# x's transposes for the second FFN in float32r, from copies of x, among its plain tiles

## The chip, the cores and the metric

One core of one Trainium2 chip runs the kernel in one launch. The metric is the device time of the launch in microseconds. The time before is the median of three runs. Four engines compute side by side, each with an instruction stream of its own in fixed order: PE multiplies, DVE and ACT work on elements, POOL issues DMAs with accumulation here; SP issues DMAs only.

## The reference

A residual layer on 512 tokens of 1024 channels, in float32:

```python
for l in range(DEPTH):
    x = x + 0.5 * swiglu_ffn(rmsnorm(x, ffn1_norm[l]), ffn1_w_gate[l], ffn1_w_up[l], ffn1_w_down[l])
    x = x + hybrid_mixer(rmsnorm(x, mix_norm[l]), w_in[l], q_norm[l], k_norm[l], rel_bias[l],
                         pool_w[l], pool_scale[l], w_out[l])
    x = x + 0.5 * swiglu_ffn(rmsnorm(x, ffn2_norm[l]), ffn2_w_gate[l], ffn2_w_up[l], ffn2_w_down[l])
    x = rmsnorm(x, final_norm[l])
return x
```

`swiglu_ffn` is `(silu(h @ w_gate) * (h @ w_up)) @ w_down` with 2816 hidden channels; `rmsnorm` divides each token by the root of its mean square and multiplies by a gain.

## The kernel before

Channels lie on the 128 partitions and tokens along the row, so x is eight tiles of 128 channels by 512 tokens, kept in SBUF. Float32 operands are split into two float32r parts, `hi` (rounded) and `lo` (the rest): `split` (lines 146 to 155) makes `hi` on ACT (line 148) and `lo` on DVE (line 149). `mm3` (lines 189 to 194) then issues three products, hi·hi at line 192, lo·hi at 193 and hi·lo at 194. The weight loads of `weights` (line 185) go out on SP, which waits at its front when a target buffer is not free.

The three parts FFN1, mixer and FFN2 follow one another. An FFN's first half is `ffn_up`. Its hidden channels are 22 tiles of 128; the first five in the order are plain, the later ones go through a Strassen scheme. The first two plain tiles are done together, gate and up of both in four PSUM banks, in four steps over the input channels called kp0 to kp3: each loads one weight tile (128 x 1024), splits it and issues 2 x 4 x 3 = 24 products. Plain tiles three and four follow one at a time, each as a gate (j = 0) and an up half (j = 1) of 24 products; these halves are called f2j0, f2j1, f3j0 and f3j1 below.

The FFN's rmsnorm is not applied to x ahead of the products. The products use x times its gain; the factor per token, `rb`, is multiplied in when the banks are emptied. It comes from `acc`, the sum of squares over tiles, which is complete when the last x tile has got the mixer's output (adds at line 1455, squares at line 304, sums at line 305). `Norm.finish` splits `acc` (lines 148 and 149), sums it over the partitions with two products against ones on PE (line 336), and goes on: square root on ACT (line 356), load of the table for silu (line 223), then on DVE `v` (line 358), reciprocal (line 359), and a Newton step (lines 360, 361, 363) that ends in `rb`. It is called within `tc.high_priority()` at the last of the kp steps; outside the manual schedules a scheduler puts each engine's stream in order when the program is built, and this priority moves its instructions forward.

FFN2's second half makes its output with tokens on the partitions, so it needs x by token, too. For that, x is transposed at the start of FFN2 (lines 1506 to 1515): eight times, four 128x128 transposes on PE from x's float32 tiles into a PSUM bank (line 1510), a copy to SBUF on ACT (line 1514), a store to the scratch `x_d` in DRAM on SP (line 1515). The second half reads it back from there much later.

`down.begin` opens the SBUF tiles for the hidden values (`acts`, one per group of hidden tiles); `open(range(G - 3))` opens all but the last three groups at once. `todo` and `piece` spread a list of small DVE and ACT tasks for the Strassen blocks among the plain tiles.

Of the kernel before, what the change touches and what calls it, by code (L numbers as in the profile page):

```python
# [1 line left out]

# [6 lines left out]
F32 = mybir.dt.float32  # L9
F32R = mybir.dt.float32r  # L10
I32 = mybir.dt.int32
AF = mybir.ActivationFunctionType
ALU = mybir.AluOpType
# [3 lines left out]
P = 128  # L17
D = 1024
S = 512
KD = D // P  # L20
NT = S // P
# [48 lines left out]
def layer(  # L70
# [31 lines left out]
    nc = tc.nc  # L102

    const = ctx.enter_context(tc.tile_pool(name="const", bufs=1))
# [13 lines left out]
    def name(what):  # L118
        n_tiles[0] += 1
        return f"{what}_{n_tiles[0]}"  # L120

    def temp(dtype=F32):
        return tpool.tile([P, S], dtype, tag="t", name=name("t"))

    def bank(tag="mm", bufs=4):
        return ps.tile([P, S], F32, tag=tag, name=name(tag), bufs=bufs)

    def abank():
        return bank("a", 4)
# [9 lines left out]
    def piece(n=1):  # L139
        for _ in range(min(n, len(todo))):  # L140
            what, *args = todo.pop(0)
            what(*args)
# [36 lines left out]
    def weights(src, parts=1):  # L179
        n = src.shape[-1]  # L180
        raw = raw_tile()
        hi, lo = part_tiles()
        for i in range(parts):
            part = slice(i * n // parts, (i + 1) * n // parts)
            nc.sync.dma_start(raw[:, part], src[:, part])  # L185
            split(raw[:, part], hi[:, part], lo[:, part])
        return hi, lo

    def mm3(acc, a, b, start, stop, further=False):

        more = dict(skip_group_check=True) if further else {}
        nc.tensor.matmul(acc, a[0], b[0], start=start, stop=False, **more)  # L192
        nc.tensor.matmul(acc, a[0], b[1], start=False, stop=False, **more)  # L193
        nc.tensor.matmul(acc, a[1], b[0], start=False, stop=stop, **more)  # L194

    def cut(pair, lo, n):
        if isinstance(pair[0], list):
            pair, lo = [z[lo // S] for z in pair], lo % S
        return pair[0][:, lo : lo + n], pair[1][:, lo : lo + n]


    def residual_tiles():
        pairs = [xpool.tile([P, 2 * S], F32, tag=f"x{k}", name=name("x")) for k in range(KD // 2)]
        return [pairs[k // 2][:, k % 2 * S : (k % 2 + 1) * S] for k in range(KD)]

    x = residual_tiles()
    x_d = dram.tile([2 * NT, P, S], F32, name="x_d")
# [3 lines left out]
    ident = const.tile([P, P], F32, name="ident")  # L211
# [3 lines left out]
    table = const.tile([P, 2], F32, name="table")  # L215
    nc.vector.memset(ones, 1.0)
    nc.vector.tensor_copy(ones_r, ones)
    eps = table[:, 1:2]
    nc.vector.memset(eps, EPS)

# [204 lines left out]
            ]  # L425


    def ffn_up(norm, wA, down, loaded):

# [6 lines left out]
        def evacuate(f, gate, up):  # L438
            g = temp()
            nc.vector.tensor_tensor(g, gate, norm.rb, op=ALU.mult)  # L440
            sg = temp()
            nc.scalar.activation(sg, g, AF.Silu)

            nc.vector.tensor_tensor(sg, sg, norm.rb, op=ALU.mult)
            down.place(f, up, sg)
            down.sums(f)
            return sg
# [3 lines left out]
        for kp in range(KD // 2):  # L451
# [10 lines left out]
            for kk in range(2):  # L462
                k = 2 * kp + kk
# [76 lines left out]
        for n, f in enumerate(down.order[2 : PLAIN - 1], 2):  # L540
            banks = []
            for j in range(2):
                wj = weights(wA[2 * f + j])
                acc = bank()
                for k in range(KD):
                    mm3(acc, cut(wj, k * P, P), norm.h[k], k == 0, k == KD - 1)
                banks.append(acc)
                piece(4)
            down.make_sums(evacuate(f, *banks), 2)
            if not loaded:  # L550
                next(consts)
        piece(len(todo) - 4)

        n, f = PLAIN - 1, down.order[PLAIN - 1]
        wj = [weights(wA[2 * f + j]) for j in range(2)]
# [43 lines left out]
        with tc.manual_schedule(engines={E.PE, E.DVE, E.Activation, E.SP}):  # L599
            last_silu = last_place = last_sums = nothing  # L600
            for n in range(PLAIN, KF):
                f = down.order[n]
                acc, up_lo, up_hi = bank()[:, :HT], bank()[:, :HT], abank()[:, :HT]
                u, z, sg = temp(), temp(), temp()
# [67 lines left out]
    groups = [(k, min(2, KH - k)) for k in range(0, KH, 2)]  # L672
    G = len(groups)

    class Down:
# [37 lines left out]
        def begin(self, pool):  # L713
            self.pool, self.acts = pool, []
            self.raws, self.parts, self.pairs = {}, {}, {}
            self.n_products, self.loads, self.loads_from = 0, [], 4
            self.open(range(G - 3))
            rooms[:] = [
                z for tag in ("ra", "rb") for z in ((wpool, "raw", RAW, 1024), (pool, tag, RAW, 2 * S))
            ]  # L720
            part_rooms[:] = [(wpool, HILO)] * HILO + [(pool, 1)]
# [116 lines left out]
    n1, n2, n3 = Norm(0), Norm(1), Norm(2)  # L838
# [11 lines left out]
    def block2(i, g):  # L850
# [6 lines left out]
    down1 = Down(  # L857
        order1, lambda f: (f % KH, f // KH), block1, RATES
    )
    down2 = Down(list(range(KF)), lambda f: (f // 2, f % 2), block2, RATES)  # L860

    with tc.tile_pool(name="act1", bufs=1, reuse_waits="tile") as apool:
        down1.begin(apool)
        ffn_up(n1, wA1, down1, loaded=False)
        p1, p5, p6 = whole(bank), whole(bank), whole(abank)

        with tc.manual_schedule(engines={mybir.EngineType.SP}):
            for g in range(G):
                down1.product(p6, g, S2, T2)
                down1.product(p1, g, A11, B11)  # L870
                down1.product(p5, g, S1, T1)
                if g == 0:

                    x[:] = residual_tiles()
                    down1.loads, down1.loads_from = [(x[k], xT[k]) for k in range(KD)], 19
        with tc.manual_schedule(engines={mybir.EngineType.SP}):
            p7 = whole(abank)
            u2 = halved(p6)

            y = [down1.acts[i // 2][:, i % 2].rearrange("p k c -> p (k c)") for i in range(2 * NT)]  # L880
            down1.product(p7, 0, S3, T3)
            for tt in range(2):
                scaled(u2[tt], p1[tt][0][0], 0.5, u2[tt], ALU.subtract)
                scaled(y[NT + 2 + tt], p5[tt][0][0], 0.5, u2[tt])
            for g in range(G):
                if g + 1 < G:
                    down1.product(p7, g + 1, S3, T3)
                down1.product(p5, g, S4, B22, further=True)

            def add(d):  # L890

                tp = bank() if d >= KD // 2 else abank()
                for t in range(NT):
                    nc.tensor.transpose(  # L894
                        tp[:, t * P : (t + 1) * P],
                        y[d // 4 * NT + t][:, d % 4 * P : (d % 4 + 1) * P], ident,
                    )
                nc.vector.tensor_tensor(x[d], x[d], tp, op=ALU.add)
                n2.add(d)

            for tt in range(2):
                todo.append((scaled, y[NT + tt], p5[tt][0][0], -0.5, u2[tt], ALU.subtract))
                todo.append((scaled, y[NT + 2 + tt], p7[tt][0][0], 0.5, y[NT + 2 + tt]))
            for g in range(G):
                down1.product(p1, g, A12, B21, further=True)
                piece()
            todo.extend((add, d) for d in range(KD // 2, KD))
            for tt in range(2):
                nc.scalar.activation(y[tt], p1[tt][0][0], AF.Copy, scale=0.5)
            ahead = down1.operands(0, A22, T4, -1.0)  # L910
            for g in range(G):
                a, w = ahead
                if g + 1 < G:
                    ahead = down1.operands(g + 1, A22, T4, -1.0)
                down1.mms(p7, g, a, w, further=True)
                piece()
            for tt in range(2):
                scaled(y[2 + tt], p7[tt][0][0], -0.5, u2[tt], ALU.subtract)
            for d in range(KD // 2):
                add(d)  # L920
        rooms[:] = [(wpool, "raw", RAW, 1024)]
# [581 lines left out]
    with tc.tile_pool(name="act2", bufs=1, reuse_waits="tile") as apool:  # L1503
        down2.begin(apool)

        for half in range(2):
            for t in range(NT):
                tp = abank()
                for j in range(4):
                    nc.tensor.transpose(  # L1510
                        tp[:, j * P : (j + 1) * P], x[4 * half + j][:, t * P : (t + 1) * P], ident
                    )
                z = temp()
                nc.scalar.copy(z, tp)
                nc.sync.dma_start(x_d[half * NT + t], z)
        ffn_up(n3, wA2, down2, loaded=True)
        xt = [hpool.tile([P, S], F32, tag="h", name=name("xt")) for _ in range(2 * NT)]
        rooms.extend((xpool, f"x{i}", 1, 2 * S) for i in range(KD // 2))
        gb = [temp(), temp()]
# [90 lines left out]
        for tt in range(2):  # L1610
            scaled(u2[tt], p1[tt][0][0], 0.5, u2[tt], ALU.subtract)
            residual(1, 2 + tt, p5[tt][0][0])
            for i in (2 + tt, NT + tt, NT + 2 + tt):
                op = ALU.subtract if i < NT + 2 else ALU.add
# [128 lines left out]
```

## Time and profile before

| what | value |
|---|---|
| median of 3 runs | 838.43 us (838.31 to 838.51) |
| the profiled execution | 838.57 us |
| its span, first to last instruction | 836.7 us |
| busy: PE, DVE, ACT, POOL | 99%, 85%, 60%, 18% |
| granted PE clock, mean | 0.997 |
| DMA, mean | 189 GB/s |

The profile is of one execution; its times in us start at the span's beginning. `a<-ident,x` reads "tile a, made from ident and x". "[0.51 <-ACT t L1514]" behind a row means that the engine stood idle for 0.51 us ahead of it, until ACT's work on t at line 1514. A row with x16 joins 16 neighbours of one line. PEld is the loading of PE's weights, which runs beside its products; SPq is SP issuing.

### The profile page before, as it was taken

The page shows a single profiled execution, that of the slowest core. Times are in us where ns is not written, and L with a number is a line of the kernel's source. Part 1 is how long each engine was busy: PE and PEld are TensorE (multiplying, and loading weights), DVE is VectorE, ACT ScalarE, POOL GpSimd, SP SyncE. Part 2 cuts the span into 40 slices and gives each one's busy share as a digit, 9 for nine tenths or more (in the row PEclk, how much of TensorE's full clock was granted, in tenths as well). Part 3 has the DMA queues.
Part 4 walks back from the last instruction along what each step waited for, and adds up shares of the span by engine and source line. Part 5 has one row for each costly group of instructions (what it writes and reads, how often), then busy time and mean ns, then how long its engine had stood idle before and what let it go on. Part 6 is the DMA issues. An engine that isn't in the chain of part 4 may idle for free.

```text
span 836.7 us, 14334 instructions
## 1 busy us (share of the span) xinstructions
PE 827.8 (99%) x5288; PEld 742.3 (89%) x5288; DVE 711.1 (85%) x1156; ACT 501.7 (60%) x859; POOL 153.1 (18%) x212
## 2 busy tenths in 40 slices
PE   9999999999999999999999999999999999999996
PEld 7889999999988888887888888889999999988885
DVE  7999999899897678767879668989889999887896
ACT  8446555665675656558747746455566555756573
POOL 0312211222073000102011000311121121132600
PEclk9999999999999999999999999999999999999998
DMA  8667788888679963332222119547877888689922
GB/s 301 194 186 200 175 211 252 191 208 205 198 239 276 336 219 111 108 110 89 75 70 64 66 55 304 173 126 215 211 214 216 217 203 209 231 268 340 325 87 101
DMA packets 77686, 158.52 MB, mean 189 GB/s; under 512 B 7200, under 2 KB 30256, under 8 KB 77232
## 3 DMA queue, kind: packets, MB, share of 16 engines
q1 hardware_dynamic: 54528, 110.93, 39.4%
q0 software_dynamic: 22656, 46.14, 26.3%
q8 instruction: 41, 0.67, 0.3%
q10 hardware_dynamic: 432, 0.54, 0.2%
q14 instruction: 29, 0.24, 0.1%
HBM read 153.38 MB, written 50.34 MB: 243 GB/s over the span
## 4 chain that ended last, share of the span: by engine, by line
PE 97%; DMA 1%; DVE 1%; SPq 0%; ACT 0%; issue 0%; DVEq 0%; ACTq 0%
PE mm L192 23%; PE mm L193 23%; PE mm L194 23%; PE a L193 8%; PE a L192 8%; PE a L194 8%; PE a L1303 1%; PE a L1239 1%; PE a L1291 1%; DMA raw<-in_wA_dram 1%; PE a L1510 0%; PE a L1161 0%; PE a L309 0%; PE a L894 0%; PE mm L894 0%; SPq L185 0%
## 5 line engine op out<-in xcount | busy, mean ns | idle before, releaser
L149 DVE TENSOR_TENSOR wlo<-raw,whi 128x1024 fp32r<-128x1024 f32 (+2 forms) x115 | 124.4, 1089 | 26.0 <-ACT whi L148 25.5
L148 ACT CAST whi<-raw 128x1024 fp32r<-128x1024 f32 (+2 forms) x115 | 107.5, 945 | 62.4 <-PE mm L193 16.9
L193 PE MATMUL mm<-ha,whi 128*128 128x256 f32 x408 | 112.9, 277 | 0.0
L192 PE MATMUL mm<-ha,whi 128*128 128x256 f32 x408 | 112.9, 277 | 0.0
L194 PE MATMUL mm<-ha,wlo 128*128 128x256 f32 x408 | 112.9, 277 | 0.0
L591 ACT ACTIVATE t<-mm 128x256 f32<-128x256 f32 x102 | 39.1, 384 | 115.2 <-PE mm L194 112.5
L495 DVE TENSOR_TENSOR wlo<-wsum,whi 128x1024 fp32r<-128x1024 f32 x68 | 83.0, 1221 | 11.2 <-PE mm L194 7.9
L732 POOL COPY mark<-t 128x1 f32<-128x1 f32 x44 | 17.5, 398 | 392.8 <-DVE t L640 242.5
L193 PEld LDWEIGHTS mm<-ha,whi 128*128 128x128 f32 x408 | 76.6, 188 | 0.1
L192 PEld LDWEIGHTS mm<-ha,whi 128*128 128x128 f32 x408 | 76.6, 188 | 0.1
L194 PEld LDWEIGHTS mm<-ha,wlo 128*128 128x128 f32 x408 | 76.6, 188 | 0.0
L192 PE MATMUL mm<-hhi,whi 128*128 128x512 f32 x192 | 75.7, 397 | 0.1
L194 PE MATMUL mm<-hhi,wlo 128*128 128x512 f32 x192 | 74.9, 392 | 0.0
L193 PE MATMUL mm<-hlo,whi 128*128 128x512 f32 x192 | 74.7, 390 | 0.0
L734 POOL DMA_DIRECT2D wsum<-in_wB_dram x72 | 71.1, 1101 | 10.4 <-issue 7.1
L490 ACT CAST whi<-wsum 128x1024 fp32r<-128x1024 f32 x68 | 67.9, 1047 | 3.3 <-DVE wsum L521 3.1
L193 PE MATMUL mm<-wlo,ah 128*128 128x512 f32 x176 | 68.7, 390 | 0.0
L194 PE MATMUL mm<-whi,ah 128*128 128x512 f32 x176 | 68.6, 390 | 0.0
L192 PE MATMUL mm<-whi,ah 128*128 128x512 f32 x176 | 68.5, 390 | 0.0
L495 DVE TENSOR_TENSOR wlo<-raw,whi 128x512 fp32r<-128x512 f32 x68 | 62.2, 951 | 0.0
L490 ACT CAST whi<-raw 128x512 fp32r<-128x512 f32 x68 | 56.3, 827 | 3.7 <-issue 2.5
L192 PE MATMUL a<-whi,ah 128*128 128x512 f32 (+1 forms) x154 | 55.8, 362 | 0.0
(229 smaller groups left out, 2399.0 us busy)
## 6 DMA issues: line engine op xcount, KB each, us to landing
raw<-in_wA_dram SPq DMA_DIRECT2D x136, 256.0 KB, 4.0
wsum<-in_wB_dram POOLq DMA_DIRECT2D x60, 512.0 KB, 7.2
raw<-wsum SPq DMA_DIRECT2D x40, 512.0 KB, 4.8
raw<-in_wB_dram SPq DMA_DIRECT2D x30, 512.0 KB, 7.2
wsum<-wsum POOLq DMA_DIRECT2D x20, 512.0 KB, 5.6
raw<-in_wA_dram SPq DMA_DIRECT2D x19, 512.0 KB, 4.8
x<-in_xT_dram SPq DMA_DIRECT2D x16, 256.0 KB, 9.0
raw<-in_wQK_dram SPq DMA_DIRECT2D x8, 512.0 KB, 3.5
```

What stands on the lines that cost most here:

```text
L148: nc.scalar.copy(hi, src)
L149: nc.vector.tensor_tensor(lo, src, hi.bitcast(F32), op=ALU.subtract)
L192: nc.tensor.matmul(acc, a[0], b[0], start=start, stop=False, **more)
L193: nc.tensor.matmul(acc, a[0], b[1], start=False, stop=False, **more)
L194: nc.tensor.matmul(acc, a[1], b[0], start=False, stop=stop, **more)
L490: nc.scalar.copy(hi, src)
L495: nc.vector.tensor_tensor(lo, src, hi.bitcast(F32), op=ALU.subtract)
L591: nc.scalar.activation(dst, src, AF.Copy, scale=scale)
L732: nc.gpsimd.tensor_copy(mark, after[:, 0:1])
L734: nc.gpsimd.dma_start(self.rows(i, g), self.rows(self.terms[i][at], g), **(dict(accum_op=ALU.add) if at else {}),)
L1239: nc.tensor.matmul(banks[i][:, at : at + n], qT[pair][0][a][rows, t * P : (t + 1) * P], kT[pair][0][b][rows, :n], start=a + b == 0, stop=a ...
L1291: nc.tensor.transpose(tp[:, n : n + P], prob[h, t][:, j * P : (j + 1) * P], ident)
```

## The change

The transposes read float32r copies of x instead of x itself. Eight DMAs on SP copy x within SBUF, bits unchanged, into two tiles `xr`, which lie in the room of the hidden values' groups 1 and 2; those groups are opened only after the plain tiles (`open(range(1))` at the start, `open(range(1, G - 3))` behind the loop), in FFN1 as well. The transposes are no longer issued at the start of FFN2 but two groups at a time at the end of each half of plain tiles three and four, through the list `further` of `ffn_up`. Each group is four float32r transposes against a float32r identity, then the copy on ACT and the store on SP. For the first group four more transposes run in float32 from the same copy; the difference of the two results times 1e9 is added to the first, on DVE.

```diff
--- before.py
+++ after.py
@@ -1,4 +1,5 @@
 from contextlib import ExitStack, nullcontext
+from functools import partial
 
 import concourse.bass as bass
 import concourse.tile as tile
@@ -215,6 +216,8 @@
     table = const.tile([P, 2], F32, name="table")
     nc.vector.memset(ones, 1.0)
     nc.vector.tensor_copy(ones_r, ones)
+    ident_r = const.tile([P, P], F32R, name="ident_r")
+    nc.vector.tensor_copy(ident_r, ident)
     eps = table[:, 1:2]
     nc.vector.memset(eps, EPS)
 
@@ -425,7 +428,7 @@
             ]
 
 
-    def ffn_up(norm, wA, down, loaded):
+    def ffn_up(norm, wA, down, loaded, further=()):
 
 
 
@@ -546,10 +549,14 @@
                     mm3(acc, cut(wj, k * P, P), norm.h[k], k == 0, k == KD - 1)
                 banks.append(acc)
                 piece(4)
+                for _ in range(2):
+                    if further:
+                        further.pop(0)()
             down.make_sums(evacuate(f, *banks), 2)
             if not loaded:
                 next(consts)
         piece(len(todo) - 4)
+        down.open(range(1, G - 3))
 
         n, f = PLAIN - 1, down.order[PLAIN - 1]
         wj = [weights(wA[2 * f + j]) for j in range(2)]
@@ -714,7 +721,7 @@
             self.pool, self.acts = pool, []
             self.raws, self.parts, self.pairs = {}, {}, {}
             self.n_products, self.loads, self.loads_from = 0, [], 4
-            self.open(range(G - 3))
+            self.open(range(1))
             rooms[:] = [
                 z for tag in ("ra", "rb") for z in ((wpool, "raw", RAW, 1024), (pool, tag, RAW, 2 * S))
             ]
@@ -861,7 +868,7 @@
 
     with tc.tile_pool(name="act1", bufs=1, reuse_waits="tile") as apool:
         down1.begin(apool)
-        ffn_up(n1, wA1, down1, loaded=False)
+        ffn_up(n1, wA1, down1, False)
         p1, p5, p6 = whole(bank), whole(bank), whole(abank)
 
         with tc.manual_schedule(engines={mybir.EngineType.SP}):
@@ -1503,17 +1510,37 @@
     with tc.tile_pool(name="act2", bufs=1, reuse_waits="tile") as apool:
         down2.begin(apool)
 
-        for half in range(2):
-            for t in range(NT):
-                tp = abank()
+        xr = [
+            apool.tile([P, 4, S], F32R, tag=f"acts{groups[g][0]}", name=name("xr")) for g in (1, 2)
+        ]
+        for k in range(KD):
+            nc.sync.dma_start(xr[k // 4][:, k % 4].bitcast(F32), x[k])
+
+        def by_token(half, t):
+
+            tp = abank()
+            for j in range(4):
+                nc.tensor.transpose(
+                    tp[:, j * P : (j + 1) * P].bitcast(F32R), xr[half][:, j, t * P : (t + 1) * P],
+                    ident_r,
+                )
+            z = temp()
+            if (half, t) == (0, 0):
+                whole_passes = abank()
                 for j in range(4):
                     nc.tensor.transpose(
-                        tp[:, j * P : (j + 1) * P], x[4 * half + j][:, t * P : (t + 1) * P], ident
+                        whole_passes[:, j * P : (j + 1) * P],
+                        xr[half][:, j, t * P : (t + 1) * P].bitcast(F32), ident,
                     )
-                z = temp()
+                differ = temp()
+                nc.scalar.copy(differ, whole_passes)
+                nc.vector.tensor_tensor(differ, tp, differ, op=ALU.subtract)
+                nc.vector.scalar_tensor_tensor(z, differ, 1e9, tp, op0=ALU.mult, op1=ALU.add)
+            else:
                 nc.scalar.copy(z, tp)
-                nc.sync.dma_start(x_d[half * NT + t], z)
-        ffn_up(n3, wA2, down2, loaded=True)
+            nc.sync.dma_start(x_d[half * NT + t], z)
+
+        ffn_up(n3, wA2, down2, True, [partial(by_token, i // NT, i % NT) for i in range(2 * NT)])
         xt = [hpool.tile([P, S], F32, tag="h", name=name("xt")) for _ in range(2 * NT)]
         rooms.extend((xpool, f"x{i}", 1, 2 * S) for i in range(KD // 2))
         gb = [temp(), temp()]
```

Line numbers of the changed kernel are higher by 1 to 7: 148 becomes 149, 336 becomes 339, 358 to 363 become 361 to 366, 1455 becomes 1462. What the scheduler makes of it stands in the engines' streams.

**PE, from the last products of the mixer** (`mm<-m`) into FFN2 (`mm<-hhi`), before:

```order
L192 MATMUL mm_5941<-m_5806,whi_5902 128x512
L193 MATMUL mm_5941<-m_5807,whi_5902 128x512
L194 MATMUL mm_5941<-m_5806,wlo_5903 128x512
L1510 MATMUL a_6043<-ident,x_3123 128x128 x2
L1510 MATMUL a_6043<-ident,x_3124 128x128 x2
L1510 MATMUL a_6051<-ident,x_3123 128x128 x2
L1510 MATMUL a_6051<-ident,x_3124 128x128 x2
L1510 MATMUL a_6059<-ident,x_3123 128x128 x2
L1510 MATMUL a_6059<-ident,x_3124 128x128 x2
L1510 MATMUL a_6067<-ident,x_3123 128x128 x2
L1510 MATMUL a_6067<-ident,x_3124 128x128 x2
L192 MATMUL mm_6107<-hhi_5896,whi_6112 128x512
```

and after the change, from the last three products of kp0 (`whi_6058`) into kp1 (`whi_6088`):

```order
L193 MATMUL mm_6056<-hhi_5917,whi_6058 128x512
L194 MATMUL mm_6056<-hlo_5918,whi_6058 128x512
L195 MATMUL mm_6056<-hhi_5917,wlo_6059 128x512
L1523 MATMUL a_6261<-ident_r,xr_6043 128x128 x4
L1531 MATMUL a_6267<-ident,xr_6043 128x128 x4
L1523 MATMUL a_6277<-ident_r,xr_6043 128x128 x4
L1523 MATMUL a_6320<-ident_r,xr_6043 128x128 x4
L193 MATMUL mm_6053<-hhi_5947,whi_6088 128x512
L194 MATMUL mm_6053<-hlo_5948,whi_6088 128x512
L193 MATMUL mm_6054<-hhi_5947,whi_6088 128x512
L194 MATMUL mm_6054<-hlo_5948,whi_6088 128x512
```

The transposes have left the front; the first 16 (12 in float32r, four in float32) stand between kp0 and kp1, and kp1 starts with eight products that need only `whi_6088`, four with `wlo_6089` behind. The other 20 stand in groups of four at the ends of f2j1 (one), f3j0 (two) and f3j1 (two).

**DVE and ACT around the norm of FFN2.** DVE before; `acc_5900` is the sum of squares, `wlo_6143` belongs to kp1 and `wlo_6173` to kp2:

```order
L149 TENSOR_TENSOR t_6208<-acc_5900,t_6207 128x512
L149 TENSOR_TENSOR wlo_6143<-raw_6141,whi_6142 128x1024
L149 TENSOR_TENSOR wlo_6173<-raw_6171,whi_6172 128x1024
L358 TENSOR_SCALAR t_6215<-a_6209 128x512
L359 RECIPROCAL t_6216<-t_6214 128x512
L149 TENSOR_TENSOR wlo_6203<-raw_6201,whi_6202 128x1024
L360 TENSOR_TENSOR t_6214<-t_6216 128x512
L149 TENSOR_TENSOR wlo_6282<-raw_6280,whi_6281 128x1024
```

DVE after the change; `t_6154` is the low part of the sum of squares, `wlo_6089` belongs to kp1:

```order
L150 TENSOR_TENSOR t_6154<-acc_5902,t_6153 128x512
L361 TENSOR_SCALAR t_6161<-a_6155 128x512
L362 RECIPROCAL t_6162<-t_6160 128x512
L363 TENSOR_TENSOR t_6160<-t_6162 128x512
L364 SCALAR_TENSOR_TENSOR t_6161<-t_6160,t_6161 128x512
L150 TENSOR_TENSOR wlo_6089<-raw_6087,whi_6088 128x1024
L366 SCALAR_TENSOR_TENSOR rb_6169<-t_6161,t_6162 128x512
L150 TENSOR_TENSOR wlo_6119<-raw_6117,whi_6118 128x1024
```

Two `wlo` stood between the norm's split and its first step; now four steps of the norm stand ahead of kp1's `wlo`. ACT before (the copy is the last of eight; `whi_6142` is kp1's):

```order
L1514 COPY t_6104<-a_6099 128x512
L148 CAST t_6207<-acc_5900 128x512
L148 CAST whi_6142<-raw_6141 128x1024
L148 CAST whi_6172<-raw_6171 128x1024
L356 ACTIVATE t_6214<-a_6209,table 128x512
L148 CAST whi_6202<-raw_6201 128x1024
L223 ACT_TABLE_LOAD
L223 ACTIVATE table<-t_6214 128x1
L148 CAST whi_6281<-raw_6280 128x1024
```

and after:

```order
L307 ACTIVATE t_6034<-x_3128 128x512
L149 CAST t_6153<-acc_5902 128x512
L359 ACTIVATE t_6160<-a_6155,table 128x512
L226 ACT_TABLE_LOAD
L226 ACTIVATE table<-t_6160 128x1
L149 CAST whi_6088<-raw_6087 128x1024
L149 CAST whi_6118<-raw_6117 128x1024
```

The copies are gone from here, and the square root and the table load now stand ahead of kp1's `whi_6088`.

**SP, from the first weights of FFN2** (`raw_6111` is kp0's, `raw_6141` kp1's, `raw_6201` kp3's), before:

```order
L185 DMA raw_6111<-in_wA_dram 128x1024
L185 DMA raw_6171<-in_wA_dram 128x1024
L185 DMA raw_6280<-in_wA_dram 128x1024
L185 DMA raw_6141<-in_wA_dram 128x1024
L185 DMA raw_6201<-in_wA_dram 128x1024
L1515 DMA x_d<-t_6048 128x512
L1515 DMA x_d<-t_6056 128x512
L1515 DMA x_d<-t_6064 128x512
```

and after (`raw_6087` is kp1's):

```order
L186 DMA raw_6057<-in_wA_dram 128x1024
L186 DMA raw_6117<-in_wA_dram 128x1024
L186 DMA raw_6226<-in_wA_dram 128x1024
L1517 DMA xr_6043<-x_3125 128x512 x2
L1517 DMA xr_6043<-x_3126 128x512 x2
L1517 DMA xr_6044<-x_3127 128x512 x2
L1517 DMA xr_6044<-x_3128 128x512 x2
L186 DMA raw_6087<-in_wA_dram 128x1024
L186 DMA raw_6147<-in_wA_dram 128x1024
```

The eight copies of x stand ahead of kp1's and kp3's weights, where the stores of x by token stood behind them; the stores now stand among the later weights.

## The prediction

> **What bounds the kernel now.** I read the page's busy table first, then the shares of the chain that ended last, and then a table by stretches of time.
>
> ```profile
> PE 827.8 (99%) x5288; PEld 742.3 (89%) x5288; DVE 711.1 (85%) x1156; ACT 501.7 (60%) x859; POOL 153.1 (18%) x212
> PE 97%; DMA 1%; DVE 1%; SPq 0%; ACT 0%; issue 0%; DVEq 0%; ACTq 0%
> ```
>
> TensorE (PE) is busy for 99% of the span and is 97% of the chain. So what counts is PE's own work and any wait put in front of it. The stretches around the start of the second FFN, and a sum over everything behind it, with the columns length, PE, PEld, DVE, ACT, POOL busy, granted clock, DMA share, GB/s:
>
> ```profile
> 502.00:510.00 8.00, 7.92 (x51) 6.50 (x50) 4.22 (x8) 7.84 (x15) 0.00 (x0) 1.00 0.86 314
> 510.00:520.00 10.00, 10.00 (x45) 8.26 (x44) 10.00 (x9) 5.83 (x7) 0.00 (x0) 1.00 0.96 320
> ```
>
> ```profile
> sum 313.00, PE 313.00 PEld 289.44 DVE 278.92 ACT 178.97 POOL 66.15; mean PE 62.60 PEld 57.89 DVE 55.78 ACT 35.79 POOL 13.23
> ```
>
> The last line sums five stretches from 515 to 828: PE is busy for all 313.00 us. Nothing there can absorb a delay: what PE loses near 510 arrives at the end in full. DVE is 10.00 of 10 busy from 510 to 520, so an instruction put ahead of another on DVE there delays the second by its whole length.
>
> **PE in the stretch that changes.** PE's timeline (start, length, what):
>
> ```profile
> 501.69 0.39 PE L194 MATMUL mm<-m,wlo 128*128 128x512 f32 x1
> 501.92 1.91 PE L1510 MATMUL a<-ident,x 128*128 128x128 f32 x16
> 503.58 0.48 PE L192 MATMUL mm<-hhi,whi 128*128 128x512 f32 x1
> 503.90 0.40 PE L193 MATMUL mm<-hlo,whi 128*128 128x512 f32 x1
> ...
> 505.06 0.66 PE L1510 MATMUL a<-ident,x 128*128 128x128 f32 x4
> 505.47 0.48 PE L194 MATMUL mm<-hhi,wlo 128*128 128x512 f32 x1
> 505.79 1.47 PE L1510 MATMUL a<-ident,x 128*128 128x128 f32 x12
> ...
> 509.76 0.44 PE L336 MATMUL a<-t,ones_r 128*128 128x512 f32 x1
> 510.04 0.39 PE L193 MATMUL mm<-hlo,whi 128*128 128x512 f32 x1
> ...
> 514.80 0.39 PE L193 MATMUL mm<-hlo,whi 128*128 128x512 f32 x1
> ```
>
> Starts tell the pace, since a printed length includes the drain. From 510.04 to 514.80 lie 21 products of 512 columns: 4.76 / 21 = 0.227 us each. The 16 transposes and the product behind them take 501.92 to 503.90; less 0.227 that is 1.75, or 0.109 per transpose, the change of type included. The lone four (505.06 to 505.79, less one product) take 0.50, 0.126 each. From 501.92 to 514.80 PE starts 37 such products and two sums of the norm beside the 32 transposes. 12.88 less 39 times 0.227 leaves 4.0 us: that is what the transposes cost now, with a stop of some 0.4 us before 505.06 and some switching.
>
> **The change, part by part.** *Removed:* the 32 transposes at the front. *Added on PE:* 36 transposes (32 in float32r, four in float32), 16 of them between the products of kp0 and kp1 (the first and second quarter of the input channels for the first two plain tiles, 24 products each), the other 20 in five groups of four, later. Does float32r change a transpose's pace? Weight loads in the attention's products, all float32r with the short 128-column forms among them, and those of the transposes now:
>
> ```profile
> 437.88 0.30 PEld L1303 LDWEIGHTS a<-pT,v 128*128 128x128 f32 x2
> ```
>
> ```profile
> L1510 PEld LDWEIGHTS a<-ident,x x32: 138/140/142, 501.7 to 506.9; 128*128 128x128 f32 x32
> ```
>
> One float32r load is 0.19 long (its rows elsewhere, as at line 192), so two in 0.30 start 0.11 apart, the pace that float32 transposes have now. No row shows a float32r transpose. From below, a matmul of 128 columns at a quarter of 0.227 would be 0.057; from above, four passes would be 0.227. I take 0.11, the load's pace.
>
> The Trainium skill ("TensorE: Matmul & The Clock Gate", "Weight-path perf modes — Fast Weight Load (FWL) and DoubleRow") says that fast weight load is on for 128 weights whenever the type is not FP32. If float32r counts as not FP32, the load would cease to be the limit, and the sum would be the fast rival's below. The row of line 1303 does not show a faster load.
>
> *Moved, the decisive part.* The eight ACT copies that stood ahead of the norm's first step go, so n3's scale is begun earlier; and on DVE that norm now stands ahead of kp1's `wlo`, which PE needs. The chain by rows of before:
>
> ```profile
> 508.25 0.68 ACT L148 CAST t<-acc 128x512 fp32r<-128x512 f32 x1
> 508.77 2.05 ACT L148 CAST whi<-raw 128x1024 fp32r<-128x1024 f32 x2
> 510.67 0.73 ACT L356 ACTIVATE t<-a,table 128x512 f32<-128x512 f32 x1
> ...
> 512.36 1.28 ACT L223 ACT_TABLE_LOAD   x1
> 513.65 0.20 ACT L223 ACTIVATE table<-t 128x1 f32<-128x1 f32 x1
> ```
>
> ```profile
> 501.44 1.37 DVE L1455 TENSOR_TENSOR x<-x,mm 128x512 f32<-128x512 f32 x2 [2.78 <-PE mm L194]
> ...
> 504.85 0.68 DVE L305 TENSOR_TENSOR acc<-acc,t 128x512 f32<-128x512 f32 x1
> 508.95 0.69 DVE L149 TENSOR_TENSOR t<-acc,t 128x512 fp32r<-128x512 f32 x1 [3.42 <-ACT t L148]
> 509.90 2.36 DVE L149 TENSOR_TENSOR wlo<-raw,whi 128x1024 fp32r<-128x1024 f32 x2 [0.26 <-ACT whi L148]
> 512.18 0.69 DVE L358 TENSOR_SCALAR t<-a 128x512 f32<-128x512 f32 x1
> 512.78 3.34 DVE L359 RECIPROCAL t<-t 128x512 f32<-128x512 f32 x1
> ...
> 517.12 0.68 DVE L360 TENSOR_TENSOR t<-t 128x512 f32<-128x512 f32 x1
> ...
> 518.85 0.69 DVE L361 SCALAR_TENSOR_TENSOR t<-t,t 128x512 f32<-128x512 f32 x1
> ```
>
> The last `acc` ends at 504.85 + 0.68 = 505.53, as now. The cast then runs to 506.2. From the cast's end to the end of the second sum takes 509.76 + 0.44 − 508.93 = 1.27, so the total is there at 507.5, the square root (0.73) at 508.25. The TENSOR_SCALAR waits for that too; RECIPROCAL starts 0.6 behind it at 508.9 and ends at 512.2; lines 360 and 361, each needing the one before, end at 512.9 and 513.6; only then comes kp1's `wlo`, 1.2: **514.8**. In before two `wlo` stood ahead of the TENSOR_SCALAR and kp1's own was finished by 511.1.
>
> On ACT, square root, table load and the one-column use of the table (508.25 + 1.28 + 0.2 = 509.7) now stand ahead of kp1's `whi` (half of 2.05): 510.75.
>
> *PE after:* 24 products and two sums from 501.92 at 0.227 end at 507.8, with 0.1 for the late second half of the sum 507.9; the 16 transposes 1.75: 509.65. **First stop** until `whi` at 510.75: 1.1. Eight products that need only `whi`, 1.8: 512.55. **Second stop** until `wlo` at 514.8: 2.25. At 514.80 PE now starts its 33rd 512-column product, where before it starts the 38th: behind by 5 × 0.227 = 1.13 us. Still to come are five groups of four, each 0.44 (4 × 0.109) to 0.50 (the lone four): 2.2 to 2.5. The four float32 transposes and twelve of the others lie ahead of the second stop and cost nothing of their own, as long as `wlo` comes last. Sum: 1.13 + 2.3 = **+3.4 us**. The other instructions (one cast of the identity early, one subtraction and one multiply-add late on DVE, 0.7 each; the ACT copies moved among the plain tiles) go to engines that run ahead of PE again: nothing, from a bound of 2 × 0.7 = 1.4 if DVE were still the last there, as it is busy for all of 510 to 520.
>
> *DMAs:* eight copies of x, 256 KB each, now stand on SP ahead of kp1's and kp3's weights; the eight stores of x by token go out later.
>
> ```profile
> 502.11 0.80 SPq L185 DMA_DIRECT2D raw<-in_wA_dram  x2
> 505.03 4.97 SPq L1515 DMA_DIRECT2D x_d<-t  x8
> ```
>
> ```profile
> L1515 SPq DMA_DIRECT2D x_d<-t x8: 320/447/757, 505.0 to 509.7; - x8
> DMA to landing us min/median/max: 2.9/3.1/3.3
> ```
>
> Stores of the same 256 KB go out one per 0.67 us (seven in 4.7) with an even landing of 3.1, so the queue kept up. The last copy needs x's last add (501.44 + 1.37 = 502.81). At 0.67 to 0.84 each (256 KB at 314 GB/s) from about 502, eight end at 507.4 to 508.7, and kp1's 512 KB at 508.7 to 510.4. `whi` may be up to 2.2 us late before the eight products run into `wlo` at 514.8, so landing up to 511.9 is free: 1.07 us per copy (511.9 − 1.34 − 502, over eight). A copy within the chip's memory is in no row of before; at twice 0.67 it would break that bound (rival below). At nothing each it would still gain nothing.
>
> The profiled run took 838.57 us (span 836.7, 1.87 outside it): 838.57 + 3.4 = 842.0. The median is 0.14 lower: **841.9**.
>
> **Rivals.** *Fast float32r:* 0.057 each; the first 16 vanish into the stops, the 20 later ones cost 1.15 and not 2.3: +2.3, 840.7. For it: half the 512-column pace; against: the load's pace. At four passes (0.227 each) the 20 cost 4.5, +5.6: 844.1.
>
> *Slow copies of x:* at 1.34 each kp1's weights land at 502 + 10.7 + 1.3 = 514.0 and `whi` is there at 515.05, `wlo` at 516.3, before the eight products are through (516.85). PE then starts its 25th product at 515.05, where before it starts the 39th: 14 × 0.227 + 2.3 = +5.5, 843.9. Against: the even landing of the stores.
>
> *The clock falls.* At the end of the kernel and at its start stand
>
> ```profile
> 4.81 1.20 PE L192 MATMUL mm<-hhi,whi 128*128 128x512 f32 x2
> 5.83 0.66 PE L193 MATMUL mm<-hlo,whi 128*128 128x512 f32 x2
> ```
>
> ```profile
> 828.77 0.28 PE L194 MATMUL a<-whi,ah 128*128 128x256 f32 x1
> ```
>
> ```profile
> 828.00:832.00 4.00, 1.05 (x9) 0.85 (x8) 3.14 (x16) 1.42 (x5) 0.00 (x0) 0.99 0.36 132
> 832.00:836.70 4.70, 0.00 (x0) 0.00 (x0) 0.61 (x1) 0.58 (x1) 0.00 (x0) 0.50 0.30 113
> ```
>
> PE's last work ends at 829.05; 0.99 over four us is half clock for 0.08, so the clock fell at 831.9, 2.9 us later. My longest stop is 2.25: it stays, if only empty time counts. At the start the products ran at half pace (0.5 each) until 5.83 though PE had work from about 1.06: 4.8 us at half would lose 2.4, so 844.3. The point is a stretch near 2.9 us without counted work.
>
> The Trainium skill ("TensorE: Matmul & The Clock Gate", "Part 4: PE-mode transpose") says that transpose mode does not count as PE being busy for the clock. Then 507.9 to 510.75, 2.85 us, would be one uncounted stretch, and this rule speaks for the rival. Before's row has the clock at 1.00 through a block of 16, which is too short to deny it.
>
> *Not slower.* RECIPROCAL, 3.34, is the largest term of the chain and has a single row. Were it 0.69 like its neighbours, `wlo` would be there at 512.2, before PE has done its eight products (512.55): the second stop goes, and +3.4 becomes +1.2, 839.6, within the bound below; with fast float32r also, 838.5. It decides at `wlo` by 512.55. Against it: the row's length with nothing to wait for; DVE is full there.
>
> **Chances.** Forecast 0.50 (own range 841.2 to 842.6); fast float32r 0.14; four passes 0.05; slow copies 0.08; clock 0.19; not slower 0.04. A run can tell about 0.2%, 1.7 us, from no change: 836.75 to 840.1. The not-slower case and the lower edge of the fast one give 0.08 for the same and 0.02 for faster; the rest, 0.90, is slower. To leave out no more than 2 in 10, the range goes from the fast case with 0.3 less (840.4) to the clock case with 0.3 more (844.6).
>
> **What would show it.** In the changed profile: PE's rows stop twice between 509 and 515, first for ACT's `whi`, then for DVE's `wlo`, about 1.1 and 2.25 long; RECIPROCAL starts near 508.9; `wlo` of kp1 ends near 514.8; the groups of four start 0.11 apart inside; kp1's weights land before 511.9; the granted clock is 1.00 from 508 to 520. No second stop, or products at half pace behind it, would make the forecast wrong.

## The result, and the profile after

The changed kernel took 843.39 us (median of four runs, 841.8 to 844.2), the kernel before 838.37 beside it: a ratio of 1.0057 with a 95% interval from 1.0040 to 1.0075. The time lies in the forecast range of 840.4 to 844.6, but not where the forecast put it (841.9). One of the four runs lay there: 841.8, at a mean granted clock of 0.997. The other three, at 0.995, took 843.37, 843.41 and 844.2. So two things have to be explained: the 3.4 us that every run lost, and the 1.6 to 2.4 us on top that most runs lost. The profiled execution is one of the second kind (843.37, span 841.6).

The page's busy table and the chain of the changed kernel look as before:

```profile
PE 829.6 (99%) x5292; PEld 743.4 (88%) x5292; DVE 712.2 (85%) x1159; ACT 501.9 (60%) x859; POOL 150.1 (18%) x212
PE 98%; DVE 1%; issue 0%; ACT 0%; DVEq 0%; ACTq 0%
```

The loss is all within 20 us. PE's timeline of the changed kernel there (start, length, what, and in brackets the idle time ahead and who ended it):

```profile
507.91 0.46 PE L1523 MATMUL a<-ident_r,xr 128*128 128x128 f32 x4
508.21 0.62 PE L1531 MATMUL a<-ident,xr 128*128 128x128 f32 x4
508.58 0.90 PE L1523 MATMUL a<-ident_r,xr 128*128 128x128 f32 x8
510.67 0.49 PE L193 MATMUL mm<-hhi,whi 128*128 128x512 f32 x1 [1.19 <-ACT whi L149]
...
512.39 0.39 PE L194 MATMUL mm<-hlo,whi 128*128 128x512 f32 x1
514.86 1.50 PE L195 MATMUL mm<-hhi,wlo 128*128 128x512 f32 x4 [2.08 <-DVE wlo L150]
516.17 0.63 PE L193 MATMUL mm<-hhi,whi 128*128 128x512 f32 x1
516.59 0.63 PE L194 MATMUL mm<-hlo,whi 128*128 128x512 f32 x1
...
518.73 0.51 PE L193 MATMUL mm<-hhi,whi 128*128 128x512 f32 x1
519.08 0.40 PE L194 MATMUL mm<-hlo,whi 128*128 128x512 f32 x1
```

Two stops, 1.19 us for kp1's high part and 2.08 us for its low part, and behind them products that start 0.43 apart (516.17, 516.59), where they start 0.227 apart at full pace. The table by stretches of the changed kernel says why; the column ahead of the last two is the granted clock:

```profile
512.00:514.00 2.00, 0.78 (x4) 0.31 (x2) 1.86 (x4) 1.46 (x2) 0.00 (x0) 1.00 0.49 199
514.00:516.00 2.00, 1.14 (x4) 0.95 (x5) 2.00 (x3) 0.00 (x0) 0.00 (x0) 0.89 0.03 10
516.00:518.00 2.00, 2.00 (x6) 1.52 (x6) 2.00 (x3) 0.00 (x0) 0.00 (x0) 0.50 0.90 283
518.00:520.00 2.00, 2.00 (x9) 1.60 (x8) 2.00 (x3) 0.00 (x0) 0.00 (x0) 0.76 0.80 273
520.00:524.00 4.00, 4.00 (x19) 3.34 (x18) 4.00 (x7) 1.06 (x1) 0.00 (x0) 1.00 0.77 249
```

The clock is halved for about 3.4 us: 0.44 in the second row (2.00 × 0.11 / 0.5), all 2.00 of the third and 0.96 of the fourth. At half pace that loses 1.7 us. By the starts above, eight products lose 0.2 us each, 1.6, which is nearly the same. The profiled times lie 4.8 us apart: stops 3.27, clock 1.7, less the 0.3 that the transposes save (from e1 below) and a gap of 0.25 that before had among them (504.59 to 505.06 less one product's pace), is 4.4; the restart behind the two stops makes the rest (512.39 to 514.86 is 2.47, which less one product's 0.227 is 2.24 and not 2.08; at the first stop it is 0.2 as well).

DVE, ACT and SP of the changed kernel, in that order, are what the forecast's chain consisted of:

```profile
508.20 0.69 DVE L361 TENSOR_SCALAR t<-a 128x512 f32<-128x512 f32 x1 [1.38 <-ACT t L359]
508.81 3.34 DVE L362 RECIPROCAL t<-t 128x512 f32<-128x512 f32 x1
512.25 0.69 DVE L363 TENSOR_TENSOR t<-t 128x512 f32<-128x512 f32 x1
512.98 0.69 DVE L364 SCALAR_TENSOR_TENSOR t<-t,t 128x512 f32<-128x512 f32 x1
513.59 1.22 DVE L150 TENSOR_TENSOR wlo<-raw,whi 128x1024 fp32r<-128x1024 f32 x1
```

```profile
507.48 0.69 ACT L359 ACTIVATE t<-a,table 128x512 f32<-128x512 f32 x1 [1.38 <-PE a L339]
508.19 1.28 ACT L226 ACT_TABLE_LOAD   x1
509.48 0.20 ACT L226 ACTIVATE table<-t 128x1 f32<-128x1 f32 x1
509.59 3.87 ACT L149 CAST whi<-raw 128x1024 fp32r<-128x1024 f32 x4
```

```profile
500.43 5.08 SPq L1517 DMA_DIRECT2D xr<-x  x8
505.62 9.55 SPq L186 DMA_DIRECT2D raw<-in_wA_dram  x5
```

DVE is in one row of work from 508.20 to 513.59, all of it the norm, while kp1's high part had been there since 510.6. kp1's weights left SP at 505.62, 3.5 us later than before (502.11), behind eight copies.

### The profile page after: what moved, and what is told of

It is laid out like the page before. It is cut to its first block, busy times and chain, and to the rows that moved or that the text cites. A ratio compares the mean times of both kernels' runs of the same rounds, so it can differ in the third digit from the quotient of the medians.

```text
span 841.6 us, 14353 instructions
## 1 busy us (share of the span) xinstructions
PE 829.6 (99%) x5292; PEld 743.4 (88%) x5292; DVE 712.2 (85%) x1159; ACT 501.9 (60%) x859; POOL 150.1 (18%) x212
## 4 chain that ended last, share of the span: by engine, by line
PE 98%; DVE 1%; issue 0%; ACT 0%; DVEq 0%; ACTq 0%
PE mm L193 23%; PE mm L195 23%; PE mm L194 23%; PE a L193 8%; PE a L194 8%; PE a L195 8%; PE a L1310 1%; PE a L1246 1%; PE a L1298 1%; PE a L232 0%; PE a L1168 0%; DVE t L362 0%; PE a L312 0%; PE mm L901 0%; PE a L901 0%; PE a L1523 0%
```

## The experiments

The theory after the result: the copies' place on SP delays kp1's weights; the scheduler's order on ACT and DVE, with the norm ahead of kp1's parts, goes with that, and together they make the two stops, 3.3 us; the rest is the halved clock, brought about by the stops. The rivals: that something else comes late behind the stops, that the copies' traffic and not their place does the harm, and, for the clock, that transposes do not count as work. Line numbers are those of each kernel.

**Late copies (e1).** The copies are issued within the first call of each half:

```diff
-        for k in range(KD):
-            nc.sync.dma_start(xr[k // 4][:, k % 4].bitcast(F32), x[k])
...
+            if t == 0:
+                for k in range(4 * half, 4 * half + 4):
+                    nc.sync.dma_start(xr[half][:, k % 4].bitcast(F32), x[k])
             tp = abank()
```

> The changed kernel, but the copies of x are issued when the first transposes of each half are called, so that they stand on SP behind the weights of kp1 and kp3; the engines' orders then put kp1's low part ahead of the norm again and all 36 transposes among the later plain tiles. If the copies' place on SP is the cause of both stops: no stop, granted clock 1.00, and before's 838.4 less 4.0 for its transposes plus 32 x 0.084 + 4 x 0.109 + some 0.4 for the changes of type = 837.9. If the loss lay in the transposes' new place among the plain tiles or in the copies' traffic, it stays at 841.8 or more.

It took 839.13 us, 1.0008 of before (0.9999 to 1.0017): both stops are gone, and so is nearly all of the loss; in the profile the clock stays at 1.00 there. It did not reach 837.9. PE's and ACT's timelines of this kernel have the reason:

```profile
507.85 0.50 PE L339 MATMUL a<-t,ones_r 128*128 128x512 f32 x1 [0.77 <-ACT t L149]
```

```profile
506.23 1.05 ACT L149 CAST whi<-raw 128x1024 fp32r<-128x1024 f32 x1 [1.90 <-DMA raw<-in_wA_dram]
507.18 0.61 ACT L149 CAST t<-acc 128x512 fp32r<-128x512 f32 x1
```

Here kp1's high part stands ahead of the norm's cast on ACT and waits for its weights; the norm's first sum on PE waits behind both, 0.77. And the transposes save less than I had put down: from the first start of each block to the product behind the one that follows, less one product's pace, they take 3.26 us, where the 32 of before take 3.57 (and a stop of 0.25 between them). A group of eight, here and in the changed kernel, lasts 0.64 to the next product's start, which itself takes 0.07 more: 0.71.

**The norm behind kp1's parts, copies still ahead (e4).** One more product, whose result is not used, is enough to make the scheduler order the engines otherwise:

```diff
+                if loaded and k == 2:
+                    filled = abank()
+                    for _ in range(1):
+                        nc.tensor.matmul(filled, w[0][:, :P], norm.h[k][0], start=True, stop=True)
```

> The changed kernel with one more product of 512 columns behind kp1's first 12, overwritten and unused; by that the engines' orders come out with kp1's low part ahead of the norm on DVE and all transposes late, while the copies of x still stand ahead of kp1's weights on SP. If the norm's place on DVE is the whole cause: about 838.1. If the copies hold up kp1's weights as well: these are issued at 505.6, land near 509.5, high part near 510.6, low part near 511.8, so PE stands still for some 3.5 to 4 us behind 507.4: 841.5 to 842 with the clock at 1.00, more if it falls.

843.65 us, 1.0067 (1.0051 to 1.0084), and PE, ACT and the stretches of this kernel show one long stop in place of two:

```profile
510.15 0.79 PE L193 MATMUL mm<-hhi,whi 128*128 128x512 f32 x1 [3.02 <-ACT whi L149]
```

```profile
509.06 3.89 ACT L149 CAST whi<-raw 128x1024 fp32r<-128x1024 f32 x4 [3.25 <-DMA raw<-in_wA_dram]
```

```profile
510.00:512.00 2.00, 1.80 (x3) 1.01 (x4) 1.86 (x2) 2.00 (x4) 0.00 (x0) 0.54 0.92 371
```

With the norm out of the way ACT waits 3.25 us for the weights themselves, until 509.06. So the copies ahead on SP cost a stop of 3.0 us by themselves, and the norm's place on DVE is not the whole cause. The order of ACT and DVE is also not bound to the copies' place: it changed here with the copies where they were. The clock fell here too, in all four runs (0.993 to 0.996), behind one stop and with the transposes far off (from 534.6).

**The copies on POOL's queue (e5).** At the same place in the program, on another queue:

```diff
-            nc.sync.dma_start(xr[k // 4][:, k % 4].bitcast(F32), x[k])
+            nc.gpsimd.dma_start(xr[k // 4][:, k % 4].bitcast(F32), x[k])
```

> The changed kernel with the copies of x issued by POOL on its own queue at the place where they stand now, so that kp1's weights no longer wait behind them on SP; their 2 MB still move at the same time. If SP's order holds kp1's weights up: these are issued near 502 and the time is that of the kernel with late copies, 839.1. If the copies' traffic does it: kp1's high part still comes near 509 to 510 and PE stands still for 2 to 3 us, 841 or more.

839.93 us, 1.0021 (1.0011 to 1.0030). ACT and PE of this kernel:

```profile
506.65 1.04 ACT L149 CAST whi<-raw 128x1024 fp32r<-128x1024 f32 x1 [2.70 <-DMA raw<-in_wA_dram]
```

```profile
508.27 0.50 PE L339 MATMUL a<-t,ones_r 128*128 128x512 f32 x1 [1.56 <-ACT t L149]
```

To set three kernels side by side: the last but one of x's squares on ACT (line 307) starts at 502.58 in e1, 502.41 in e4 and 502.20 in e5. Counted from there, kp1's weights are at hand after 3.65 us in e1, 6.65 in e4 and 4.45 in e5, where the same 2 MB move at the same time as in e4. The queue's order is the larger part, 2.2 of the 3.0 us; the traffic is 0.8, by which the stop ahead of the norm's sum grows from 0.77 to 1.56. The profile of e5 has one more wait, 0.8 for a low part late in the second half of FFN2, whose cause was not looked into.

**Filling the stops (e2, e3, e10).** Products whose operands have long been in place are put ahead of the first 16 transposes, 13 or 5 of them; what they write is overwritten by the transposes. The orders of all engines are otherwise those of the changed kernel:

```diff
+            for _ in range(13 if (half, t) == (0, 0) else 0):
+                nc.tensor.matmul(tp, ones_r, n3.h[0][0], start=True, stop=True)
```

> The changed kernel with 13 more products of 512 columns, whose result is overwritten, ahead of its first 16 transposes: 2.95 us of work within the 3.3 us in which PE stood still. The engines' orders are otherwise those of the changed kernel. If the time beyond 841.8 is the halved clock that the stops bring: clock 1.00 through, 841.8 in every run, no spread. If it is something else that comes late behind the stops: 843.4 as before, and half pace behind kp1's low part again.

841.75 us (841.32 to 842.02, four runs, all at clock 0.997), 1.0042. PE has 2.95 us more to do, and the median falls by 1.6. The wait (us in total, times, longest) and the stretch of this kernel:

```profile
PE mm L195 <- DVE wlo L150: 0.4, 1, 0.4
```

```profile
514.00:516.00 2.00, 1.56 (x8) 1.06 (x7) 2.00 (x3) 0.00 (x0) 0.00 (x0) 1.00 0.19 29
```

`wlo` comes when it came, the clock stays at 1.00, and the excess over 841.8 is gone. The excess is the clock.

> As the one with 13, but five products: they fill the first stop (1.19 us) alone, the second (2.1 us) stays. If the second stop alone makes the clock fall: 843 to 844, with spread. If it takes both stops and the uncounted transposes between them: 841.8.

842.01 us (841.28 to 843.79, four runs), the second stop left at 2.0:

```profile
PE mm L195 <- DVE wlo L150: 2.0, 1, 2.0
```

One of the four runs had the lower clock (843.79, 0.996). Since four runs say little of a share, this kernel and the changed one were run again, side by side (e9, e10):

> The kernel with five more products (first stop filled, second of 2.0 us left), more often: if the second stop alone is enough, as many runs lie near 843.5 as of the changed kernel; if the first stop counts as well, clearly fewer (one of four so far).

841.8 us (840.82 to 843.45, five runs), all five at 0.997.

> The changed kernel itself, more often, for the spread: if the clock falls or not by where the two stops meet the windows in which it is judged, a few runs stay near 841.8 with clock 0.997 or more, and most lie 1.5 to 2.5 higher with 0.996 or less.

843.36 us (841.44 to 844.3, five runs); four at 0.995 and one, the 841.44, at 0.997. By the mean clock (0.996 or less) the changed kernel lost its clock in 7 of 9 runs, the one with the first stop filled in 1 of 9, the one with both filled in none of 4. The middle count is not firm. The 843.45 of e10, at 0.997, lies as high as a run that lost its clock; and the mean also moves with the length of the kernel's end at half clock: the profiles of before and e5 keep 1.00 until PE's last work is done and have means of 0.997 and 0.999. In the profile of the repeated run the clock falls later against the stop than in the first:

```profile
515.54 1.20 PE L195 MATMUL mm<-hhi,wlo 128*128 128x512 f32 x4 [2.08 <-DVE wlo L150]
516.57 0.39 PE L193 MATMUL mm<-hhi,whi 128*128 128x512 f32 x1
516.80 0.52 PE L194 MATMUL mm<-hlo,whi 128*128 128x512 f32 x1
517.12 0.63 PE L195 MATMUL mm<-hhi,wlo 128*128 128x512 f32 x1
...
520.11 0.50 PE L193 MATMUL mm<-hhi,whi 128*128 128x512 f32 x1
```

PE starts again at 515.54 and runs at full pace until 516.9; only then do the products come 0.43 apart, until 520.3: 3.4 us again.

**The moments of the fall, from the traces.** The records of the granted clock in the traces of the changed kernel, e9 and e4 have it fall at 515.55, 516.92 and 510.16, and each time it is back 3.41 us later. In them it first rose near the kernel's start, at 6.96, 4.92 and 4.99. Between rise and fall lie 508.59, 512.00 and 505.17 us, which is 149, 150 and 148 times 3.413. So in these traces the clock changed only at marks that are 3.413 us apart, and where the marks lie against the program differs from run to run. Cut at the marks, the stretches with the fall at their end are these, of the changed kernel, e9 and e4 in turn (the second number is PE's busy time):

```profile
512.13:515.55 3.42, 1.34 (x6) 0.79 (x5) 3.28 (x6) 1.33 (x2) 0.00 (x0) 1.00 0.25 101
513.50:516.92 3.42, 1.38 (x6) 1.16 (x7) 3.38 (x5) 0.64 (x1) 0.00 (x0) 1.00 0.21 55
506.75:510.16 3.41, 0.39 (x3) 0.01 (x1) 0.03 (x1) 1.10 (x2) 0.00 (x0) 1.00 0.98 353
```

PE stood still in them for 2.08, 2.04 and 3.02 us. The first stop lies in the stretch before (508.72 to 512.13 in the changed kernel, 1.19 idle), and no fall stands at its end. In e3's profile, without a fall, a mark cuts the second stop of 2.05 in two, and the emptiest stretch has 1.74 idle:

```profile
513.06:516.47 3.41, 1.67 (x7) 1.42 (x8) 3.41 (x5) 0.34 (x1) 0.00 (x0) 1.00 0.16 41
```

In e10's profile, again without a fall, the two parts are 1.04 and 1.06. So no profile shows that the two stops add up: the second alone was enough where it fell between two marks. If that is all, the second stop should bring the fall in four to six runs of ten, in e3 and e10 as in the changed kernel. That is an estimate: of 3.41 us for the place of a mark, 3.41 − 2.08 = 1.33 leave the stop whole, and twice 0.33 more leave at least 1.75 of it. Counts of 7 in 9 and of 1 or 2 in 9 lie far apart for that, so a part of the first stop is not excluded.

**Transposes and the clock (e7).** The kernel before with its transposes four times over:

```diff
-                for j in range(4):
-                    nc.tensor.transpose(
+                for _ in range(4):
+                    for j in range(4):
+                        nc.tensor.transpose(
```

> The kernel before with each block of transposes at the start of the second FFN issued four times over, 64 in an unbroken row of 7 us and 128 in all: 96 x 0.109 = 10.5 us more, 848.9, if transposes count as work for the clock (1.00 from 500 to 525). If they do not count, the granted clock falls to a half within the row, and the time is 850 or more.

849.2 us in its one run. PE's timeline and a stretch of this kernel:

```profile
502.52 14.13 PE L1511 MATMUL a<-ident,x 128*128 128x128 f32 x128
```

```profile
514.00:516.00 2.00, 2.00 (x21) 2.00 (x20) 0.00 (x0) 0.59 (x1) 0.00 (x0) 1.00 0.84 280
```

All 128 came in one row of 14 us (I had reckoned with two rows), and the clock is 1.00 to its end at an unchanged 0.109 each (13.97 / 128). The Trainium skill ("TensorE: Matmul & The Clock Gate", "Part 4: PE-mode transpose") says that transpose mode does not count as PE being busy in the same way as other work. These float32 transposes keep the clock up all the same; a row of float32r transposes as long was not run.

**The type alone (e6).** The kernel with late copies, its transposes in float32 from the same copies:

```diff
-                    tp[:, j * P : (j + 1) * P].bitcast(F32R), xr[half][:, j, t * P : (t + 1) * P],
-                    ident_r,
+                    tp[:, j * P : (j + 1) * P], xr[half][:, j, t * P : (t + 1) * P].bitcast(F32),
+                    ident,
```

> The kernel with late copies (839.13), with all 36 transposes in float32 from the same copies. If float32r sets the pace (0.084 against 0.109 per transpose, by the changed profile): 32 x 0.025 = 0.8 more, 839.9. If the load of the weights or something beside the type sets it: no change, 839.1.

840.15 us (1.0019, 1.0010 to 1.0028) against 839.13: slower by 1.0, in runs that spread by 2.9 us. Its profile is the surer measure. A group of eight in float32 here, and in the changed kernel in float32r, each with the product behind it:

```profile
539.42 1.03 PE L1524 MATMUL a<-ident,xr 128*128 128x128 f32 x8
540.22 0.48 PE L193 MATMUL mm<-hhi,whi 128*128 128x512 f32 x1
540.53 0.39 PE L194 MATMUL mm<-hlo,whi 128*128 128x512 f32 x1
```

```profile
547.82 0.80 PE L1523 MATMUL a<-ident_r,xr 128*128 128x128 f32 x8
548.46 0.46 PE L193 MATMUL mm<-hhi,whi 128*128 128x512 f32 x1
548.76 0.39 PE L194 MATMUL mm<-hlo,whi 128*128 128x512 f32 x1
```

540.53 − 539.42 less 0.227 is 0.88; 548.76 − 547.82 less 0.227 is 0.71. So a float32r transpose saves 0.17 / 8 = 0.021 us, and 32 of them 0.7. The rest of the 1.0 need not be the type's, since runs differ already ahead of FFN2: its first product starts at 503.66 in this profile and at 501.70 in e1's.

**Late and lean (e8).** Late copies, without the four float32 transposes and the added difference (left out of what is computed), and with the sum of squares cast on DVE, which stood idle there:

```diff
-            split(self.acc, *pair)
+            nc.vector.tensor_copy(pair[0], self.acc)
+            nc.vector.tensor_tensor(pair[1], self.acc, pair[0].bitcast(F32), op=ALU.subtract)
...
-            if (half, t) == (0, 0):
+            if False:
```

> The kernel with late copies, without the four float32 transposes and the added difference (left out of the computation), and with the sum of squares cast on DVE, which is idle there, so that it does not queue behind kp1's high part on ACT. Less 0.77 for the stop ahead of the norm's first sum, less 0.44 for four transposes: 839.1 - 1.2 = 837.9, half a microsecond below before, if those two are all that is left; 838.5 if the cast's place does not matter.

838.36 us, 0.9999 of before (0.9990 to 1.0007). The stop ahead of the norm's sum is gone (no wait of PE is left in the second FFN's first part), and the time comes down by 0.8 from e1, not by 1.2. It equals before within what can be told. Within FFN2 the profile does have the half microsecond: from PE's first instruction of FFN2 to the start of the last product pass 326.41 us (502.11 to 828.52), and 326.85 in before (501.92 to 828.77). In the medians it does not show. The spread from ahead of FFN2 is as large: its start differs by 0.68 between two profiles of one and the same kernel (501.82 and 502.50 for the changed one).

## Why the prediction was right, and where it was not

- *PE bounds, and nothing behind 515 absorbs a delay:* right. The two kernels' last products start at 828.77 and 833.64, 4.9 us apart, and the profiled times lie 4.8 apart.
- *The chain on DVE:* right to some 0.1 us in each step: RECIPROCAL forecast at 508.9 and found at 508.81, `wlo` ready at 514.8 and found at 513.59 + 1.22 = 514.81. *On ACT:* `whi` forecast for 510.75, PE went on at 510.67. First stop 1.1 against 1.19, second 2.25 against 2.08.
- *Transposes:* the pace of float32r was mis-sized, 0.11 taken and 0.08 found (0.64 / 8). The weight load's pace was not the limit that I took it for. The 20 later ones cost 0.37 + 0.71 + 0.71 = 1.8 and not 2.3, by the blocks of the changed kernel. The fast rival's 0.057 was too low.
- *Copies:* eight at 0.6 on SP, landing 2.6 us after issue; kp1's weights were in time for ACT, whose table use ended at 509.68. The rival of slow copies did not occur. But I treated their place on SP as free up to 511.9, and so it was only because the norm stood in front anyway: e4 has the weights themselves as what is waited for.
- *The sum without the clock:* +3.4 forecast; the two runs of the changed kernel that kept their clock took 841.8 and 841.44, which is +3.4 and +2.8 against the befores beside them (838.37, 838.64). By the rows it is +3.0: the 33rd product starts at 514.86, 1.2 behind before's, and the later transposes take 1.8. With 1.7 for the clock that makes 4.7 of the 4.8.
- *The clock:* this step failed. The prediction said that "my longest stop is 2.25: it stays, if only empty time counts", measured against the 2.9 us that pass at the kernel's end before the clock falls, and gave the fall a chance of 0.19. It fell in 7 of 9 runs. By the prediction's own sign, products at half pace behind the second stop, the forecast's account is wrong for those. What the runs show in its place: 2.04 us of standing still between two marks were enough. The 2.9 us at the kernel's end were no bound but the way to the next mark; in e10 the same way is 2.3 us (831.37 to 833.65) and in e3 5.1 (832.22 to 837.32). The rival's own price, 2.4, was too high: 1.7 in the profile (3.4 us at half pace), as the kernel's start takes longer to get its clock (4.8 us) than a running kernel to get it back.
- *The range:* it held 843.39 only because the clock's rival set its upper end, and that is in part luck. The reason that spoke for the rival, transposes that do not count, is not borne out: in e4 the clock falls with no transposes near, in e2 it stays up with the same 16 transposes there, and in e7 it stays up through 128 of them.

What stays open: how long PE may stand still between two marks (2.04 us was too long, 1.74 was not), and whether the first stop adds to the second, as the counts suggest and no profile shows. The Trainium skill ("TensorE: Matmul & The Clock Gate", "What's actually happening") gives a free-running window of about 3.4 us, which agrees with the 3.413 us between marks and with a fall whose moment the program does not set. Its condition, an idle window, does not: no stretch of 3.4 us was idle ahead of these falls. That the norm's place on DVE would cost its own stop with the copies late was not tried either; it is read from DVE's rows.

## What to carry to other kernels

A copy put ahead of weights on a queue can cost twice: the weights come late, and the scheduler's order on the other engines may come out anew, as it did here; look at what now stands ahead of the first consumer on every engine, not only at the queue. When a change brings PE to a stand for about 2 us within 3.4, count a halved clock (here 1.7 us lost) as a likely case, and one that differs from run to run: it came in 7 of 9 runs with a longest stop of 2.08 us and in all four with one of 3.02. Moving work into the place that a stop leaves is free only until the stop itself is removed: here the transposes' saving, 0.3 us in all, was a tenth of what the stops took.

## What the runs showed of the hardware

- The clock fell with a longest stop of 2.08 us, up to 1.4 us after PE had gone back to work, and stayed at a half for 3.41 us.
- In three traces the clock's first rise and its fall lie 148, 149 and 150 times 3.413 us apart. PE had stood still for 2.04 to 3.02 of the last 3.41 us ahead of each fall; after 1.74 us of it (e3) the clock stayed up.
- Thirteen useless products in front of the wait made the kernel 1.6 us faster (843.39 to 841.75), since the clock stayed up.
- Float32 transposes of 128 x 128 kept the clock at 1.00 for 14 us.
- A transpose took 0.109 us in float32 and 0.08 in float32r within a row.
